# The rotary split of head group 0 in the four softmax buffers, and half of the second gated unit ahead of the first attention

## The chip, the cores and the metric

The kernel runs on one core of one Trainium2 chip, as one program. The metric is the device time of a run in microseconds (us); of several runs the median counts. Lower is better.

## What is computed

The reference is a two-layer backbone over 1024 latent tokens and 256 context tokens, 1024 channels wide. Layer 0 mixes with mLSTM heads and Fourier groups, layer 1 with differential attention and a convolution module; behind each mixer stands a squared-ReLU feed-forward part. The change lies in layer 1's mixer:

```python
q, k, v, glu = jnp.split(h @ w_in, [D_C, 2 * D_C, 3 * D_C], axis=-1)
ql = apply_rope(ql, cos, sin); kl = apply_rope(kl, cos, sin)
s = jnp.einsum('bqhmd,bkhmd->bhmqk', q, k) * (DIFF_DH ** -0.5)      # m = 0, 1: two maps per head
a = softmax(s)[:, :, 0] - lam * softmax(s)[:, :, 1]
o = jnp.einsum('bhqk,bkhd->bqhd', a, v)                             # then an RMS norm per head
a, gte = jnp.split(glu, 2, axis=-1)
z = depthwise_conv(a * jax.nn.sigmoid(gte), w_dw)                   # 31 taps; then layer norm and silu
```

There are six heads, each with two maps of 64 channels and a value of 128. Queries are the 1024 latent tokens, keys and values those and the 256 context tokens.

## The kernel before, in words

**Numbers.** Float32 products are made from pairs: an operand is split into a high part `hi` (rounded to the float32r type) and a low part `lo = x - hi`, and one product is three matmuls (hi by hi, hi by lo, lo by hi: L129, L130, L131). A product over 1024 channels is 8 x 3 = 24 matmuls into one accumulator bank `acc`, of which there are three. Activations are kept as pairs for three token blocks (512, 512 and 256 tokens). Weights come in by SP's queue (`st`, three buffers, L97), ScalarE makes `wah` (L110) and VectorE `wal` (L111).

**Heads in groups.** The six heads are done in three groups of two. For a group, `rope_proj` (its lines are L1016 and on) makes K and then Q. For each token block it makes two products, one for each half of the rotation pairs (A and B). For the latent blocks VectorE then does six operations on the two banks: L1035 (A times cosine), L1036 (B times sine), L1037 (their difference: half 0 is ready), L1038 (A times sine: bank A is read for the last time), L1039 (B times cosine: bank B is free) and L1041 (their sum: half 1 is ready). The tables of cosine (`rc`) and sine (`rs`) have one buffer each, and are loaded anew for each block (L1033, L1034).

**The split.** `to_stack` splits a finished half: ScalarE writes `hi` (L1011), VectorE `lo` (L1012), and SP stores each to a scratch tensor in DRAM, `kd` or `qd` (L1014). The tag `rh` has two buffers for all of this, one pair. A store of a block of 512 tokens is 256 KB, with a destination of 4 x 32 x 512.

**Attention.** `attention` loads K (L1072, 640 KB a map, three buffers) and Q (L1077) back from the scratch. For each block of 128 queries it makes S for both maps (L1086: two matmuls for each of three stretches of keys), the maxima (L1088, L1091), the exponentials into the buffers `p0` and `p1` (L1094; two of each, 1280 columns), the weighted difference (L1101), ten transposes (L1107), the product with the values (L1112), a norm, and a store (L1125).

**The convolution module.** `glu(m)` loads two weight tiles and makes the gated unit of 128 channels: for each of the two latent blocks a product for the gate, a tanh (L969), a product for the value, and their product into `u` (L971). `conv` is one VectorE operation and 30 more over 1024 columns (L976, L978).

**What sets the order.** The kernel is written once, in order; a scheduler then deals the instructions to the engines' queues by a model of their times, so later matmuls stand between those of a stage that waits. Each engine works through its queue in order, and SP's queue, which issues all of these DMAs, stops at a DMA whose data are not there. The written order here is: values of group 0, `glu(0)`, K and Q of group 0, `conv(0)`, attention of group 0, `glu(1)`, K and Q of group 1, values of group 1, `conv(1)`, attention of group 1, and so on.

Of the kernel before, what the change touches and what calls it, by code (L numbers as in the profile page):

```python
# [10 lines left out]
F32R = mybir.dt.float32r  # L11
# [6 lines left out]
P = 128  # L18
# [3 lines left out]
NTOK = T_LAT + T_CTX  # L22
# [20 lines left out]
def body(tc, A, out):  # L43
    with ExitStack() as es:
        trunk(tc, es, A, out)
# [6 lines left out]
def trunk(tc, es, A, out):  # L52
# [12 lines left out]
    def f(ap):  # L65
        return ap.bitcast(F32)
# [13 lines left out]
    def acc(w=512):  # L80
        t = psa.tile([P, 512], F32, tag="acc", name="acc")
        return t[:, :w]
# [31 lines left out]
    def wload(src, shape, pl=None, tag="wa", bufs=3):  # L114
        return wsplit(wstage(src, shape), shape, pl, tag, bufs)
# [20 lines left out]
    def proj(ps, w, h, order=range(KT)):  # L136

        for n, k in enumerate(order):
            mm3(ps, (w[0][:, k, :], w[1][:, k, :]), h[k], n == 0, n == KT - 1)
# [200 lines left out]
    with ExitStack() as em, eg:  # L340
# [57 lines left out]
        for src, dst in ((LI, RI), (LF, RF)):  # L398
            for c0 in range(0, NCH, 4):
                n = min(4, NCH - c0)  # L400
# [428 lines left out]
    with ExitStack() as ef:  # L829
# [30 lines left out]
        for fo in range(5):  # L860
            w = ws[fo] if fo < 2 else wload(A["w_out0"][fo], (KT, P))
            for tb in (0, 1, 2):
                o, n = TBS[tb]
# [65 lines left out]
    pc = er.enter_context(tc.tile_pool(name="proj1", bufs=1, side="right", reuse_waits="tile"))  # L929
# [23 lines left out]
    def hk(tb):  # L953
        return [h1[k, tb] for k in range(KT)]
# [3 lines left out]
    def glu(m):  # L958
        wg = wload(A["w_glu"][2 + m], (KT, P))
        wa = wload(A["w_glu"][m], (KT, P))  # L960
        u = pc.tile([P, T_LAT + 30], F32, tag="uz", bufs=3, name="uz")
        nc.any.memset(u[:, 0:15], 0.0)
        nc.any.memset(u[:, T_LAT + 15:], 0.0)
        for tb in (0, 1):
            o = TBS[tb][0]
            pg_, pa_ = acc(), acc()
            proj(pg_, wg, hk(tb))
            t = pc.tile([P, 512], F32, tag="rt", bufs=3, name="rt")
            act.activation(t, pg_, AF.Tanh, scale=0.5)  # L969
            proj(pa_, wa, hk(tb))  # L970
            dve.scalar_tensor_tensor(u[:, 15 + o:15 + o + 512], t, 1.0, pa_, ADD, MUL)  # L971
        return u

    def conv(m, u):
        zm = pc.tile([P, T_LAT + 30], F32, tag="uz", bufs=3, name="uz")[:, 0:T_LAT]
        dve.tensor_scalar(zm, u[:, 0:T_LAT], dwh[:, m:m + 1], None, MUL)  # L976
        for j in range(1, 31):
            dve.scalar_tensor_tensor(zm, u[:, j:j + T_LAT], dwh[:, 2 * j + m:2 * j + m + 1], zm, MUL, ADD)  # L978
        z.append(zm)
# [26 lines left out]
        yield  # L1006

    def to_stack(dst, g, half, t, o, n, sc):
        hi = pc.tile([P, 512], F32R, tag="rh", bufs=2, name="rh")[:, :n]
        lo = pc.tile([P, 512], F32R, tag="rh", bufs=2, name="rh")[:, :n]  # L1010
        act.activation(hi, t, AF.Copy, scale=sc)  # L1011
        dve.scalar_tensor_tensor(lo, t, sc, f(hi), MUL, SUB)  # L1012
        for kind, s in ((0, hi), (1, lo)):
            sp.dma_start(f(dst[g, :, kind, half, :, o:o + n]), f(s))  # L1014

    def rope_proj(g, q):  # L1016
        w = [wload(A["w_qk1"][q, g, half], (KT, P)) for half in range(2)]
        dst, sc = (kd, 1.0) if q else (qd, 0.125)
        for tb in ((0, 1, 2) if q else (0, 1)):
            o, n = TBS[tb]  # L1020
            pA, pB = acc(n), acc(n)
            proj(pA, w[0], hk(tb))
            proj(pB, w[1], hk(tb))
            t = [pc.tile([P, 512], F32, tag="rt", bufs=3, name="rt")[:, :n] for _ in range(3 if tb < 2 else 2)]
            if tb == 2:
                act.copy(t[0], pA)
                act.copy(t[1], pB)
                to_stack(dst, g, 0, t[0], o, n, sc)
                to_stack(dst, g, 1, t[1], o, n, sc)
                yield  # L1030
                continue
            c_, s_ = (pc.tile([P, 512], F32, tag=x, bufs=1, name=x) for x in ("rc", "rs"))
            sp.dma_start(c_, A["rope"][0, :, o:o + n])  # L1033
            sp.dma_start(s_, A["rope"][1, :, o:o + n])  # L1034
            dve.tensor_mul(t[0], pA, c_)  # L1035
            dve.tensor_mul(t[1], pB, s_)  # L1036
            dve.tensor_sub(t[2], t[0], t[1])  # L1037
            dve.tensor_mul(t[0], pA, s_)  # L1038
            dve.tensor_mul(t[1], pB, c_)  # L1039
            to_stack(dst, g, 0, t[2], o, n, sc)  # L1040
            dve.tensor_add(t[0], t[0], t[1])  # L1041
            to_stack(dst, g, 1, t[0], o, n, sc)
            yield

    def v_proj(g):
        wv = [wload(A["w_v1"][g][:, a:a + 4, :], (4, 256)) for a in (0, 4)]
        v = {}
        for c in (0, 1, 2, 3, 8, 9, 4, 5, 6, 7):
            tb, off = tok(c)
            ps = acc(256)  # L1050
            for kk in range(KT):
                w = wv[kk // 4]
                mm3(ps, tuple(t[:, off:off + P] for t in h1[kk, tb]),
                    (w[0][:, kk % 4, :], w[1][:, kk % 4, :]), kk == 0, kk == KT - 1)
            vt = pv.tile([P, 256], F32, tag="v", bufs=13, name="v")
            act.copy(vt, ps)
            v[c] = vt
        return v
# [69 lines left out]
    pt = e1.enter_context(tc.tile_pool(name="att", bufs=1, reuse_waits="tile"))  # L1128
    def qk_proj1(g):
        for q in (1, 0):  # L1130
            for _ in rope_proj(g, q):
                pass

    v = v_proj(0)
    u = [glu(0)]
    qk_proj1(0)
    conv(0, u[0])
    for _ in attention(0, v, False):
        pass
    u.append(glu(1))  # L1140
    qk_proj1(1)
    v = v_proj(1)
    conv(1, u[1])
    for _ in attention(1, v, False):
        pass
    parts = {"K": rope_proj(2, 1), "Q": rope_proj(2, 0), "0": layernorm_silu(0), "1": layernorm_silu(1)}
# [338 lines left out]
    for j in range(3, 15):  # L1485
        u = up_unit(j)
        u.run(*WORDER)
        u.store()
    u = up_unit(15, False, LORDER)
# [39 lines left out]
    for seg in segs:  # L1529
        tb, a, n = seg  # L1530
# [87 lines left out]
```

## Time and profile before

| | us |
|---|---|
| median of 3 runs | 3104.14 |
| lowest and highest | 3098.87, 3105.69 |
| the profiled execution's own time | 3095.96 |
| its span, from the first to the last instruction | 3094.2 |

The profile is of one execution; times in it are us from the span's start. TensorE is PE, its weight loads PEld, VectorE DVE, ScalarE ACT, GpSimd POOL, and SP issues the DMAs. A row of a timeline has start, duration, engine, line, operation, and in brackets the idle time before it with what ended it; matmuls overlap, so their pace is read from their starts. DMA share is the mean busy share of the core's 16 DMA engines.

### The profile page before, as it was taken

How to read it: one execution, taken by the hardware profiler on the slowest of the kernel's cores; microseconds unless marked ns; L12 is line 12 of the kernel's file. 1: busy time of each engine (PE TensorE's matmuls, PEld its weight loads, DVE VectorE, ACT ScalarE, POOL GpSimd, SP SyncE). 2: the span in 40 equal slices, each digit the busy share in tenths (PEclk: the TensorE clock that was granted, in tenths of full speed). 3: DMA queues.
4: the chain of work that ended last, by engine and by line, in shares of the span. 5: the costliest groups of instructions: out<-in, count | busy, mean ns of one | idle time of the engine just before them, and what ended most of it. 6: DMA issues, size and time to landing. Idle time of an engine off the chain costs nothing.

```text
span 3094.2 us, 44658 instructions
## 1 busy us (share of the span) xinstructions
PE 2933.4 (95%) x16386; PEld 2461.5 (80%) x16386; DVE 1959.3 (63%) x3885; ACT 1205.1 (39%) x2660; POOL 306.0 (10%) x483
## 2 busy tenths in 40 slices
PE   6899999999999999999999799999999799989998
PEld 5787878788888888888888677877877578867787
DVE  6859696646456544544446788567567776657666
ACT  3335354433321222222233145566666454433332
POOL 0002011001122222222100000000000000000000
PEclk9999999999999999999999899999999899999999
DMA  6143334551244444444321333232613386697751
GB/s 214 45 155 108 111 115 136 175 180 55 96 150 158 157 151 141 170 157 164 129 83 63 112 108 109 80 89 82 197 60 109 110 275 233 231 306 236 240 178 65
DMA packets 303803, 443.52 MB, mean 143 GB/s; under 512 B 25712, under 2 KB 174816, under 8 KB 303584
## 3 DMA queue, kind: packets, MB, share of 16 engines
q1 hardware_dynamic: 300992, 436.74, 43.4%
q10 hardware_dynamic: 2592, 3.93, 0.4%
q8 instruction: 129, 2.11, 0.3%
q14 instruction: 90, 0.74, 0.1%
HBM read 330.08 MB, written 110.49 MB: 142 GB/s over the span
## 4 chain that ended last, share of the span: by engine, by line
PE 73%; DVE 11%; DMA 9%; POOL 2%; ACT 2%; issue 2%; SPq 1%; POOLq 0%; DVEq 0%; ACTq 0%
PE acc L131 11%; PE acc L129 11%; PE acc L130 11%; PE acc L1314 8%; PE bd L1314 6%; PE ff L129 4%; PE ff L130 4%; PE ff L131 4%; PE po L1112 3%; PE S L1086 3%; DMA st<-in_ff_dram 2%; DMA kd<-rh 2%; PE pT L1107 2%; DMA qd<-rh 1%; DMA t<-sw 1%
## 5 line engine op out<-in xcount | busy, mean ns | idle before, releaser
L129 PE MATMUL acc<-a,wah 128*128 128x512 f32 (+1 forms) x1752 | 650.1, 371 | 22.4 <-DVE rt L1038 14.1
L130 PE MATMUL acc<-a,wah 128*128 128x512 f32 (+1 forms) x1752 | 644.6, 368 | 0.0
L131 PE MATMUL acc<-a,wal 128*128 128x512 f32 (+1 forms) x1752 | 643.4, 368 | 0.0
L129 PEld LDWEIGHTS acc<-a,wah 128*128 128x128 f32 x1752 | 336.0, 192 | 72.2 <-DVE rt L1038 14.7
L131 PEld LDWEIGHTS acc<-a,wal 128*128 128x128 f32 x1752 | 336.0, 192 | 47.5 <-DVE wal L111 0.6
L130 PEld LDWEIGHTS acc<-a,wah 128*128 128x128 f32 x1752 | 336.2, 192 | 45.6 <-issue 0.5
L110 ACT CAST wah<-st 128x1024 fp32r<-128x1024 f32 (+4 forms) x129 | 120.4, 935 | 483.2 <-DMA st<-in_ff_dram 375.1
L129 PE MATMUL ff<-s,wbh 128*128 128x512 f32 (+1 forms) x768 | 274.3, 359 | 0.2 <-DVE x L710 0.2
L130 PE MATMUL ff<-s,wbh 128*128 128x512 f32 (+1 forms) x768 | 272.4, 355 | 0.0
L131 PE MATMUL ff<-s,wbl 128*128 128x512 f32 (+1 forms) x768 | 271.6, 354 | 0.0
L111 DVE TENSOR_TENSOR wal<-st,wah 128x1024 fp32r<-128x1024 f32 (+4 forms) x129 | 139.3, 1083 | 202.9 <-ACT wah L110 202.6
L710 DVE SCALAR_TENSOR_TENSOR x<-ff,mod,x 128x512 f32<-128x512 f32 (+1 forms) x264 | 171.0, 658 | 96.1 <-PE ff L131 94.8
L1088 DVE TENSOR_REDUCE mx<-S 128x1 f32<-128x512 f32 (+1 forms) x288 | 165.6, 594 | 68.8 <-PE S L1086 67.3
L1094 ACT ACTIVATE p<-S,nm 128x512 f32<-128x512 f32 (+1 forms) x288 | 176.0, 620 | 45.7 <-DVE nm L1091 45.4
L1086 PE MATMUL S<-K,Q 128*128 128x512 f32 (+1 forms) x576 | 164.6, 386 | 15.7 <-ACT p L1094 7.1
L753 DVE TENSOR_TENSOR s<-s,s 128x512 fp32r<-128x512 f32 (+1 forms) x96 | 64.7, 680 | 167.9 <-ACT s L752 167.8
L1314 PE MATMUL bd<-a,wbh 128*128 128x512 f32 x480 | 153.9, 401 | 15.6 <-ACT wbh L1265 8.5
L129 PE MATMUL acc<-wah,a 128*128 128x256 f32 (+1 forms) x560 | 161.8, 290 | 6.5 <-ACT a L271 4.1
L129 PEld LDWEIGHTS ff<-s,wbh 128*128 128x128 f32 x768 | 144.8, 189 | 24.5 <-DVE x L710 1.0
L130 PEld LDWEIGHTS ff<-s,wbh 128*128 128x128 f32 x768 | 145.2, 189 | 20.7 <-DVE s L753 0.6
L131 PEld LDWEIGHTS ff<-s,wbl 128*128 128x128 f32 x768 | 144.9, 189 | 20.8
L131 PE MATMUL acc<-wah,a 128*128 128x256 f32 (+1 forms) x560 | 159.6, 290 | 0.3 <-DVE a L272 0.2
(391 smaller groups left out, 5913.1 us busy)
## 6 DMA issues: line engine op xcount, KB each, us to landing
st<-in_ff_dram SPq DMA_DIRECT2D x168, 256.0 KB
st<-in_ff_dram SPq DMA_DIRECT2D x68, 512.0 KB
st<-in_w_mod_dram SPq DMA_DIRECT2D x48, 512.0 KB
a<-sw SPq DMA_DIRECT2D x84, 256.0 KB
stm<-in_w_mod_dram SPq DMA_DIRECT2D x128, 128.0 KB
su<-st SPq DMA_DIRECT2D x32, 512.0 KB
bc<-rb SPq DMA_DIRECT2D x30, 512.0 KB
sv<-st SPq DMA_DIRECT2D x28, 512.0 KB
```

What stands on the lines that cost most here:

```text
L110: act.copy(hi, v)
L111: dve.tensor_sub(lo, v, f(hi))
L129: pe.matmul(ps, lh, rh, start=first, stop=False)
L130: pe.matmul(ps, lh, rl, start=False, stop=False)
L131: pe.matmul(ps, ll, rh, start=False, stop=last)
L710: dve.scalar_tensor_tensor(xt, ps, mod[:, self.l, ch, fo, s:s + 1], xt, MUL, ADD)
L753: dve.tensor_sub(lo, r, f(hi))
L1086: pe.matmul(s_, Q[m][:, kind, qb * P:(qb + 1) * P], K[hh, m][:, a:a + n], start=(kind == 0), stop=(kind == 1))
L1088: dve.tensor_reduce(mx[:, i:i + 1], s_, AX, MAX)
L1094: act.activation(e[:, a:a + n], S[i], AF.Exp, bias=nm, accum_out=Z[:, m, i:i + 1])
L1112: pe.matmul(po[:, 0:P], aT[:, (c - c0) * P:(c - c0 + 1) * P], v[c][:, hh * P:(hh + 1) * P], start=(c == 0), stop=(c == NCH - 1))
L1314: pe.matmul(ps, l_, r_, start=bool(first) and j == 0 and i == 0, stop=j == n - 1 and i == 2, skip_group_check=True)
```

## The change

`to_stack` takes its pair, for group 0 only, from the attention's buffers `p0` (half 0) and `p1` (half 1): a buffer of 1280 columns holds `hi` in its first n columns and `lo` from column 512 on. So group 0 has four pairs, two for each half, instead of one. Groups 1 and 2 keep `rh`. And `glu` hands out its tile after each token block, so that the main order can run it in two parts: the first block of `glu(1)` is now written ahead of the attention of group 0, the second behind it.

```diff
-        return u
+            yield u
...
     def to_stack(dst, g, half, t, o, n, sc):
-        hi = pc.tile([P, 512], F32R, tag="rh", bufs=2, name="rh")[:, :n]
-        lo = pc.tile([P, 512], F32R, tag="rh", bufs=2, name="rh")[:, :n]
+        if g == 0:
+            hl = pt.tile([P, NTOK], F32R, tag=f"p{half}", bufs=2, name="rp")
+            hi, lo = hl[:, :n], hl[:, 512:512 + n]
+        else:
+            hi, lo = (pc.tile([P, 512], F32R, tag="rh", bufs=2, name="rh")[:, :n] for _ in range(2))
         act.activation(hi, t, AF.Copy, scale=sc)
         dve.scalar_tensor_tensor(lo, t, sc, f(hi), MUL, SUB)
...
     v = v_proj(0)
-    u = [glu(0)]
+    *_, u0 = glu(0)
     qk_proj1(0)
-    conv(0, u[0])
+    conv(0, u0)
+    g1 = glu(1)
+    next(g1)
     for _ in attention(0, v, False):
         pass
-    u.append(glu(1))
+    u1 = next(g1)
     qk_proj1(1)
     v = v_proj(1)
-    conv(1, u[1])
+    conv(1, u1)
```

In the changed file the lines of `to_stack`, `rope_proj` and `attention` have numbers higher by 3: L1038 becomes L1041, L1014 becomes L1017.

TensorE's order around the first S of group 0. The names `a_154..` are activations of token block 0, `a_158..` of block 1; the rows here are of the half unit's products. Two places of the difference:

```order
 L129 MATMUL acc<-a_15496,wah 128x512
 L130 MATMUL acc<-a_15497,wah 128x512
-L1086 MATMUL S<-K,Q 128x512 x2
-L1086 MATMUL S<-K,Q 128x256
 L131 MATMUL acc<-a_15496,wal 128x512
 L129 MATMUL acc<-a_15447,wah 128x512
...
 L131 MATMUL acc<-a_15496,wal 128x512
+L1089 MATMUL S<-K,Q 128x512 x4
+L1089 MATMUL S<-K,Q 128x256 x2
 L129 MATMUL acc<-a_15823,wah 128x512
 L130 MATMUL acc<-a_15824,wah 128x512
```

The first S matmuls stood inside the half unit, three of them one matmul before the end of its first product and three in the middle of its second (34 of its 48 matmuls are ahead of those); now both products are done before the first S.

SP's order from K's last stores to the loads of Q, before:

```order
L1014 DMA kd<-rh 4x32x256 x4
L1072 DMA K<-kd 128x1280 x2
L1014 DMA qd<-rh 4x32x512 x2
L1033 DMA rc<-in_rope_dram 128x512
L1034 DMA rs<-in_rope_dram 128x512
L1014 DMA qd<-rh 4x32x512
L1072 DMA K<-kd 128x1280
L1014 DMA qd<-rh 4x32x512
L1077 DMA Q<-qd 64x512 x3
```

and now:

```order
L1017 DMA kd<-rp 4x32x256 x4
L97 DMA st<-in_w_qk_dram 128x1024 x2
L1075 DMA K<-kd 128x1280 x3
L1017 DMA qd<-rp 4x32x512
L1037 DMA rs<-in_rope_dram 128x512
L1036 DMA rc<-in_rope_dram 128x512
L1017 DMA qd<-rp 4x32x512 x3
L1080 DMA Q<-qd 64x512 x6
```

The third K load has moved up to the first two, ahead of the first store of Q and of the tables for Q's second block; two weight loads stand ahead of them all.

VectorE's order for K's token block 1, now:

```order
L1015 SCALAR_TENSOR_TENSOR rp<-rt,rp 128x512
L1038 TENSOR_TENSOR rt<-acc,rc 128x512
L978 SCALAR_TENSOR_TENSOR uz<-uz,dwh 128x1024 x2
L1039 TENSOR_TENSOR rt<-acc,rs 128x512
L978 SCALAR_TENSOR_TENSOR uz<-uz,dwh 128x1024
L1040 TENSOR_TENSOR rt<-rt 128x512
L978 SCALAR_TENSOR_TENSOR uz<-uz,dwh 128x1024
L1041 TENSOR_TENSOR rt<-acc,rs 128x512
```

Before, one convolution step (L978) stood between the first two of these rotary operations, and two ahead of the split in the first row; now it is two and one.

## Rows read from the trace of the kernel before

**Rows 1.** The page's first section: busy us, share of the span and instructions of each engine.

```profile
PE 2933.4 (95%) x16386; PEld 2461.5 (80%) x16386; DVE 1959.3 (63%) x3885; ACT 1205.1 (39%) x2660; POOL 306.0 (10%) x483
```

**Rows 2.** Busy time by stretch: from:to, us, busy us of each engine (instructions), granted TensorE clock as a share of full speed, DMA share, GB/s.

```profile
1700.00:1800.00 100.00, 78.23 (x335) 64.55 (x334) 67.03 (x77) 14.48 (x26) 0.00 (x0) 0.88 0.38 121
...
1800.00:2390.00 590.00, 559.60 (x3419) 468.30 (x3418) 421.45 (x895) 365.18 (x1030) 40.13 (x51) 0.99 0.33 102
```

**Rows 3.** TensorE's timeline from the end of K's last product to the first attention block; the bracket holds the idle time before a row and what ended it.

```profile
1726.81 0.28 PE L130 MATMUL acc<-a,wah 128*128 128x256 f32 x1
1726.93 0.28 PE L131 MATMUL acc<-a,wal 128*128 128x256 f32 x1
1734.63 0.58 PE L129 MATMUL acc<-a,wah 128*128 128x256 f32 x1 [7.42 <-DVE rt L1038]
...
1735.23 0.41 PE L131 MATMUL acc<-a,wal 128*128 128x256 f32 x1
1735.44 0.41 PE L129 MATMUL acc<-a,wah 128*128 128x256 f32 x1
...
1763.38 0.80 PE L129 MATMUL acc<-a,wah 128*128 128x512 f32 x1 [6.67 <-DVE rt L1038]
...
1764.40 0.63 PE L131 MATMUL acc<-a,wal 128*128 128x512 f32 x1
1764.83 0.63 PE L129 MATMUL acc<-a,wah 128*128 128x512 f32 x1
...
1782.83 1.41 PE L1086 MATMUL S<-K,Q 128*128 128x512 f32 x3 [6.49 <-DMA Q<-qd]
...
1788.73 0.75 PE L1086 MATMUL S<-K,Q 128*128 128x512 f32 x3
1789.31 0.39 PE L131 MATMUL acc<-a,wal 128*128 128x512 f32 x1
1789.54 0.40 PE L129 MATMUL acc<-a,wah 128*128 128x512 f32 x1
...
1798.61 0.73 PE L1086 MATMUL S<-K,Q 128*128 128x512 f32 x2 [1.18 <-ACT p L1094]
```

**Rows 4.** Who waited for whom in 1716 to 1800, TensorE and then VectorE: us in total, times, longest.

```profile
PE acc L129 <- DVE rt L1038: 14.1, 2, 7.4
...
DVE rh L1012 <- DMA qd<-rh: 12.9, 3, 5.6
DVE rh L1012 <- DMA kd<-rh: 11.8, 4, 5.8
```

**Rows 5.** The chain of waits that ended last, in order of time: start, us, what.

```profile
1719.12 8.68 DMA kd<-rh
...
1764.55 8.10 DMA qd<-rh
```

**Rows 6.** Busy time by short stretch, columns as in rows 2; the last two are DMA share and GB/s.

```profile
1721.00:1722.00 1.00, 1.00 (x6) 0.84 (x5) 1.00 (x1) 0.00 (x0) 0.00 (x0) 1.00 0.43 154
1722.00:1723.00 1.00, 1.00 (x6) 0.84 (x5) 0.10 (x1) 0.00 (x0) 0.00 (x0) 1.00 0.26 88
1723.00:1724.00 1.00, 1.00 (x6) 0.81 (x6) 0.00 (x0) 0.00 (x0) 0.00 (x0) 1.00 0.35 121
1724.00:1725.00 1.00, 1.00 (x9) 0.96 (x8) 0.00 (x0) 0.63 (x1) 0.00 (x0) 1.00 0.25 98
...
1750.00:1752.00 2.00, 2.00 (x10) 1.66 (x9) 0.00 (x0) 0.00 (x0) 0.00 (x0) 1.00 0.26 101
...
1764.00:1766.00 2.00, 2.00 (x6) 1.62 (x5) 2.00 (x3) 0.00 (x0) 0.00 (x0) 0.50 0.99 392
```

**Rows 7.** VectorE's timeline at K's token block 1; a convolution step (L978) and a rotary operation give their pace by the next start.

```profile
1719.50 2.60 DVE L978 SCALAR_TENSOR_TENSOR uz<-uz,dwh 128x1024 f32<-128x1024 f32 x2
1727.90 0.69 DVE L1012 SCALAR_TENSOR_TENSOR rh<-rt,rh 128x512 fp32r<-128x512 f32 x1 [5.81 <-DMA kd<-rh]
1728.51 0.68 DVE L1035 TENSOR_TENSOR rt<-acc,rc 128x512 f32<-128x512 f32 x1
1729.11 1.28 DVE L978 SCALAR_TENSOR_TENSOR uz<-uz,dwh 128x1024 f32<-128x1024 f32 x1
```

**Rows 8.** The timeline of SP's queue, which issues the DMAs: start and us of the issuing (not of the transfer).

```profile
1716.68 0.61 SPq L1014 DMA_DIRECT2D kd<-rh  x1
...
1718.41 0.66 SPq L1033 DMA_DIRECT2D rc<-in_rope_dram  x1
...
1761.27 0.81 SPq L1072 DMA_DIRECT2D K<-kd  x2
...
1777.97 1.80 SPq L1077 DMA_DIRECT2D Q<-qd  x3
```

**Rows 9.** ScalarE's timeline: the split of half 1 of K's token block 0, which waits for the store of half 0.

```profile
1724.05 0.63 ACT L1011 ACTIVATE rh<-rt 128x512 fp32r<-128x512 f32 x1 [7.40 <-DMA kd<-rh]
```

**Rows 10.** Whom TensorE waited for in 1800 to 2390: us in total, times, longest.

```profile
PE po L1121 <- ACT ob L1120: 9.9, 11, 2.2
PE pT L1107 <- DVE p L1101: 6.3, 4, 2.9
PE S L1086 <- ACT p L1094: 5.9, 6, 2.1
...
PE acc L986 <- DVE rt L1038: 0.7, 1, 0.7
```

## The prediction

> **What bounds the kernel now.** The page's first section puts TensorE at 95% of the span [rows 1], so a change can only gain where TensorE stands still or runs at the low clock. The busy table by stretch says where that is near this change: in 1700 to 1800 us TensorE is busy 78.23 of 100 us at a mean granted clock of 0.88; in 1800 to 2390, the rest of the attention part, it is busy 559.60 of 590 at 0.99 [rows 2]. So the stretch is 1700 to 1800: the rotary projections of group 0 and the start of its attention.
>
> TensorE's timeline there shows four stops: 7.42, 6.67, 6.49 and 1.18 us [rows 3]. After each long one the matmuls start at the lower of the two clock levels: 128x256 matmuls then follow each other by 0.21 us instead of 0.12, 128x512 ones by 0.43 instead of 0.23 [rows 3]. The slow stretches hold 24 of the narrow ones after the first stop, some 10 wide ones after the second and 11 wide plus three S products after the third: 2.2 + 2.0 + 2.4 = 6.6 us. Stops and low clock together are 21.8 + 6.6 = 28.4 us.
>
> Who is waited for: twice VectorE's L1038 [rows 3, 4], once the load of Q, once an exponential [rows 3]. VectorE itself sits 24.7 us in L1012 (11.8 and 12.9) until a store to kd or qd lands [rows 4]. The chain of waits runs store after store, 8.1 to 8.7 us each from issue to landing [rows 5]: with two "rh" buffers, one hi/lo pair, the next half can't be split before the last pair has landed. L1038 frees an accumulator bank, so TensorE stands still behind that chain.
>
> **What the change does here, step by step.** No matmul, VectorE or ScalarE operation is added or taken away; buffers and order change. I step through the new order with durations from the rows: a rotary operation holds VectorE 0.60 us, a convolution step 1.20 [rows 7], 24 wide matmuls take 24 x 0.227 = 5.4 us, 24 narrow ones 2.9 at full clock.
>
> *K, token block 1 (first stop).* Before, L1035 of block 1 started at 1728.51, right after the split that waited for the store until 1727.90 [rows 7]. Now the split of half 1 has its own pair, and VectorE is free at about 1721. It then waits for something else: the rotary tables have one buffer each, and are reloaded behind the first hi store, the second of them at 1718.41 [rows 8]. When they land no row says. Bounds: 1721 (VectorE free) and 1728.5 (L1035 ran then). Near the lower end would need tables that pass the store; the DMA share says otherwise: it is 0.43 from 1721, then 0.26, 0.35, and from 1724 on 0.25 with 98 GB/s, which is what a store alone shows [rows 6]. So I take 1725. From there to the end of L1041 (today's L1038) it is four rotary operations and four convolution steps, 7.3 us: 1732.4. TensorE, out of work at 1727.2, stands 5.2 us instead of 7.4, with 2.2 us of low clock after.
>
> *Q, token block 0 (second stop).* TensorE now ends K at 1737.5 (24 narrow at 0.21), Q block 0 at 1748.4, the first half of Q block 1 at 1753.8, and then wants the bank that L1041 of Q block 0 frees. VectorE starts that block at 1743.2 (the first product is there at 1742.9) and needs 4 x 0.60 + 6 x 1.20 = 9.6 us: 1752.8. The stop goes, and its 2.0 us of low clock; 1.0 us is to spare.
>
> *Half a gated unit (third stop).* Q block 1 ends at 1759.3, the first product of the half unit at 1764.7. The second wants the bank of L1041 of Q block 1, and that waits for the tables again. On SP they now stand behind three K loads, and these wait for all twelve kd stores. A lone store shows 256 KB at 101 GB/s with a DMA share of 0.26 [rows 6], so 2.6 us each once they stand in a row; on the quarter of the engines that it uses, a table takes 0.65. The first store of K block 1 goes out at about 1731.2, behind L1040 and its copy on ScalarE, and lands 7.4 later, as the very first did (issued at 1716.68, waited for until 1724.05) [rows 8, 9]: 1738.6; two tables, three stores of 256 KB and four of 128 KB behind it are 1.3 + 7.8 + 5.2: 1752.9. Three K loads of 640 KB at 392 GB/s [rows 6] take 5.0, with 1.5 until the engines fill: 1759.5. A qd store and the two tables, 3.9: 1763.4. L1038 to L1041 with three convolution steps and one weight split, 7.1: 1770.5. So TensorE stands 5.9 us, now in the half unit, and loses 2.0 more at the low clock: 1778.0.
>
> *First S.* Behind the tables three qd stores land by 1771.2. Today S starts 4.9 us after the first load of Q was issued (1777.97 and 1782.83) [rows 3, 8]: 1776.1, before 1778.0. No wait, with 1.9 to spare. The six S matmuls end at 1779.2. Today the same work, projections, half a unit and the first S, ends at 1792.3: the last three S matmuls start at 1788.73, thirteen wide ones follow [rows 3]. That is **13.1 us** earlier. The 1.18 us behind it goes too: today the three maxima of S stand between convolution steps on VectorE; now they follow each other.
>
> *The rest of attention.* The order is dealt anew to the end of group 2's attention, with the same work. TensorE's waits there are 30.4 us in 590 [rows 2], the largest for the squares and the copy of the output block (9.9), the weighted difference (6.3) and the exponential (5.9) [rows 10]; for an accumulator it waits 0.7. The half unit taken ahead leaves less cover there, but only 14 of its 48 matmuls stood behind the first S products before: 3.2 us. I put the sum at no change and its bounds at 6 us either way.
>
> **Sum.** 13.1 + 1.2 = 14.3 us. The profiled execution took 3095.96 us (span 3094.2), so it would become 3081.7; it lies 8.2 below the median of the runs, 3104.14. From the median: **3089.8 us**. A measurement here tells about 0.2% (6.2 us) from no change.
>
> **The rivals.**
> *A, the burst of stores buys nothing* (0.16). The stores share their quarter of the engines, so twelve issued early may end no earlier than today, when the K loads went out at 1761.27 [rows 8]. Then the tables land at 1772.5, L1041 at 1779.6, and the third stop becomes 15 us. Stops and clock are 24.4 instead of 15.3, the gain 5: 3099. For it: where only stores run the share is 0.25 or 0.26 [rows 6]. Against: today VectorE waits between them [rows 4].
> *B, the tables come early* (0.07). If stores held nothing up, the first stop would shrink to 1.3 us, VectorE would reach Q block 1 in time, and nearly all of 28.4 us would come back: some 26, 3078. Against it: 8.1 to 8.7 us a store [rows 5] and the quarter share [rows 6]. In the Trainium skill, DMA: Bandwidth & Descriptors, section Anatomy of one DMA, the fit of 2.0 us plus bytes over 436 GB/s (measured on the GpSimd path) would give an estimate of 2.6 us for such a store from issue to landing, and with it this rival's time. The same page of the Trainium skill, section Why a DMA increments its semaphore by 16 and not by 1, has a copy run on as many of the 16 engines as divide the slowest dimension of both sides, four for a destination of 4x32x512; the share of 0.26 agrees, and by that the sum is mine.
> *C, attention waits more* (0.13). The same order that fills the start leaves the blocks behind less covered; if the 30.4 us grow by a quarter, 7.6, the gain is 6.7: 3097. For it: 7,869 rows of TensorE's order differ. Against: only 3.2 us of cover move.
> *D, slower: stores in a row don't overlap* (0.04). SP stops at the K loads until the last kd store lands, and qd stores, tables and loads of Q stand behind. If each 256 KB took the 8.7 us of the chain's rows even in a burst, kd would end at about 1804, the tables would land at 1815 and the half unit end at 1829, 51 us after my 1778: some 37 slower, 3141. It decides from where five such stores' time (three whole, four half) eats 14.3 us: (13.0 + 14.3) / 5 = 5.5 us each. Against it: from 1724 to 1725 a quarter of the engines was still at 98 GB/s when the first store had landed and the next was in flight [rows 6, 9], so the next had not waited for it.
> That the order doesn't do what was meant is excluded by its rows: both products of the half unit stand ahead of the first S.
>
> **How the numbers follow.** My forecast has 0.60, with a range of its own of 3084 to 3096: gains of 8 to 20, from the tables' bounds (2 to 4 us each way), the 1.0 and 1.9 us to spare, and 6 us in attention. For 8 in 10 the range takes in A and C: **3080 to 3101**; beyond it are D, much of B and the ends of the others. Faster by over 0.2%: nearly all of the forecast, B, and parts of A and C, 0.70. Within: the rest of A and C, 0.25. Slower: D and a rough attention, 0.05.
>
> **What would show it.** Right: VectorE no longer waits for kd or qd in the splits; TensorE's second stop is gone, one of about 5 us stays ahead of K's last product and one of 5 to 6 stands inside the half unit, released by L1041; first S near 1778; no store-by-store chain. Wrong: a stop of 10 us or more in the half unit (A), none (B), waits of 36 us or more behind 1800 (C), K loads after 1765 (D).

## The result, and the profile after

The changed kernel takes **3086.1 us** (median of 5 executions, 3081.27 to 3089.09) against 3104.14 (3098.87 to 3105.69): ratio 0.9946, 95% interval 0.9931 to 0.9960, so 16.8 us faster (12 to 21). The forecast was 14.3 us faster, 3089.8. Measured once more, beside the later experiments, it took 3084.15, ratio 0.9948 (0.9933 to 0.9962).

The two profiled executions differ by less, 3095.96 and 3086.10, since the one of before lies 8 us below its own median. They also reach the changed stretch at different times, with the same instructions ahead of it. I therefore count between two points that both have, called marks here. The first mark is the first store to kd (1716.68 before [rows 8], 1720.30 after). The second is the end of SP's issuing of the attention's last output store, ha. That second mark, in SP's timeline of before:

```profile
2381.37 8.18 SPq L1125 DMA_DIRECT2D ha<-oo  x2
```

and of after, with the other issues that count here (start, us of issuing):

```profile
1720.30 0.61 SPq L1017 DMA_DIRECT2D kd<-rp  x1
...
1757.20 1.27 SPq L1075 DMA_DIRECT2D K<-kd  x3
1759.70 0.44 SPq L1036 DMA_DIRECT2D rc<-in_rope_dram  x1
...
2371.05 8.21 SPq L1128 DMA_DIRECT2D ha<-oo  x2
```

From mark to mark it is 672.87 us before and 658.96 after: **13.9 us** of gain, all of it in this part. Behind the second mark 704.7 us are left before and 705.1 after. The busy table from mark to mark, before and then after (start:end, length, busy us and instructions of TensorE, weight load, VectorE, ScalarE, GpSimd, granted clock, DMA share, GB/s):

```profile
1716.68:2389.55 672.87, 620.70 (x3675) 518.66 (x3674) 474.22 (x957) 377.41 (x1052) 40.13 (x51) 0.97 0.34 106
```

```profile
1720.30:2379.26 658.96, 615.21 (x3675) 514.38 (x3674) 474.60 (x957) 379.07 (x1052) 44.90 (x51) 0.98 0.34 108
```

The same 3675 recorded matmuls stand in both. TensorE's idle time falls from 52.2 to 43.75 us, 8.4 less, and the matmuls themselves take 5.5 us less, at a mean granted clock of 0.98 instead of 0.97. Together these are the 13.9.

TensorE's timeline of after in the changed stretch, with all its stops of over 0.5 us and the first S (in brackets: idle time, and what ended it), answers to [rows 3]:

```profile
1736.58 0.58 PE L129 MATMUL acc<-a,wah 128*128 128x256 f32 x1 [5.74 <-DVE rt L1041]
...
1776.82 0.77 PE L129 MATMUL acc<-a,wah 128*128 128x512 f32 x1 [7.31 <-DVE rt L1041]
...
1783.83 1.31 PE L1089 MATMUL S<-K,Q 128*128 128x512 f32 x6
...
1790.23 0.63 PE L1089 MATMUL S<-K,Q 128*128 128x512 f32 x2
```

Four stops of 21.8 us have become two of 13.05. The first S waits for nothing, nor do the next ones up to 1800. Who is waited for in 1716 to 1800, against [rows 4] (us, times, longest):

```profile
PE acc L129 <- DVE rt L1041: 13.1, 2, 7.3
...
DVE rt L1038 <- DMA rc<-in_rope_dram: 12.2, 2, 8.0
```

VectorE's 24.7 us of waiting for stores in the split are gone. In their place it waits for the rotary tables, twice, and its timeline shows that these two waits stand ahead of TensorE's two stops:

```profile
1729.13 0.69 DVE L1038 TENSOR_TENSOR rt<-acc,rc 128x512 f32<-128x512 f32 x1 [4.12 <-DMA rc<-in_rope_dram]
...
1747.79 0.69 DVE L1038 TENSOR_TENSOR rt<-acc,rc 128x512 f32<-128x512 f32 x1
...
1769.46 0.69 DVE L1038 TENSOR_TENSOR rt<-acc,rc 128x512 f32<-128x512 f32 x1 [8.04 <-DMA rc<-in_rope_dram]
```

The rest of the attention, from behind the first S products to the second mark, against the last 590 us of [rows 2]:

```profile
1790.00:2379.00 589.00, 558.30 (x3422) 466.47 (x3420) 421.84 (x894) 366.37 (x1030) 44.90 (x51) 0.99 0.33 103
```

TensorE is idle for 30.7 us there, before for 30.4 in 590.

### The profile page after: what moved, and what is told of

Read it like the earlier page. It is cut to its first block, busy times and chain, and to the rows that moved or that the text cites. A ratio compares the mean times of both kernels' runs of the same rounds, so it can differ in the third digit from the quotient of the medians.

```text
span 3084.4 us, 44653 instructions
## 1 busy us (share of the span) xinstructions
PE 2931.9 (95%) x16386; PEld 2461.1 (80%) x16386; DVE 1957.8 (63%) x3885; ACT 1207.1 (39%) x2660; POOL 310.1 (10%) x483
## 5 line engine op out<-in xcount | busy, mean ns | idle before, releaser
L129 PE MATMUL acc<-a,wah 128*128 128x512 f32 (+1 forms) x1752 | 649.6, 371 | 22.0 <-DVE rt L1041 13.1
L1089 PE MATMUL S<-K,Q 128*128 128x512 f32 (+1 forms) x576 | 161.5, 379 | 11.5 <-ACT p L1097 11.5
L130 PE MATMUL acc<-wal,a 128*128 128x256 f32 (+1 forms) x560 | 161.8, 290 | 0.0
```

Source lines behind the costliest of these rows:

```text
L129: pe.matmul(ps, lh, rh, start=first, stop=False)
L130: pe.matmul(ps, lh, rl, start=False, stop=False)
L1089: pe.matmul(s_, Q[m][:, kind, qb * P:(qb + 1) * P], K[hh, m][:, a:a + n], start=(kind == 0), stop=(kind == 1))
```

## The experiments

Gain below is one less the ratio, times the median of before in the same batch (3104.14 for the change; 3101.61 for e1, e2, e3 and e5; 3100.84 for r, e4, e6 and e7; 3101.11 for e8 to e11). "Mark to mark" and the idle time of TensorE in it come from each run's one profiled execution. They tell where time went; for how much, the medians count: the changed kernel's two traces agree to 0.2 us, but e2's is 3.8 us longer than that of before, though its median is 1.9 us lower. In the runs with four-part stores in the later groups, 10 or 13 matmuls more than the 3675 lie between the marks, since the second mark falls later in TensorE's order there (in e8 and e9 that is 2 to 3 us of TensorE's work).

| run | median us | ratio (95%) | gain us | mark to mark | TensorE idle |
|---|---|---|---|---|---|
| before | 3104.14 | | | 672.9 | 52.2 |
| the change | 3086.10 | 0.9946 (0.9931 to 0.9960) | 16.8 | 659.0 | 43.8 |
| r_after_again | 3084.15 | 0.9948 (0.9933 to 0.9962) | 16.1 | 658.8 | 43.8 |
| e1_buffers | 3093.87 | 0.9974 (0.9963 to 0.9984) | 8.1 | 669.6 | 49.9 |
| e2_half | 3099.46 | 0.9994 (0.9986 to 1.0003) | 1.9 | 676.7 | 53.1 |
| e3_tables | 3080.13 | 0.9929 (0.9916 to 0.9942) | 22.0 | 657.5 | 41.1 |
| e5_before_spread | 3087.79 | 0.9951 (0.9939 to 0.9964) | 15.2 | 657.1 | 39.7 |
| e4_after_spread | 3082.65 | 0.9941 (0.9926 to 0.9956) | 18.3 | 655.9 | 36.7 |
| e7_after_spread_first | 3090.83 | 0.9968 (0.9957 to 0.9980) | 9.9 | 665.4 | 44.6 |
| e6_tables_spread | 3080.39 | 0.9934 (0.9919 to 0.9949) | 20.5 | 655.6 | 36.8 |
| e8_after_spread_later | 3069.59 | 0.9895 (0.9882 to 0.9909) | 32.6 | 647.0 | 29.4 |
| e9_tables_spread_later | 3067.03 | 0.9888 (0.9875 to 0.9902) | 34.7 | 641.5 | 25.8 |
| e10_before_spread_first | 3087.48 | 0.9951 (0.9937 to 0.9964) | 15.2 | 658.4 | 46.8 |
| e11_before_spread_later | 3091.04 | 0.9967 (0.9955 to 0.9980) | 10.2 | 662.9 | 42.0 |

My theory was that one store of a hi or lo half holds the only buffer pair, that the splits therefore run store after store, and that with more buffers the tables behind the stores hold next. The main rival was that it is the work order (half a unit ahead) that gains, or that the stores hold nothing.

**e1_buffers**: the four softmax buffers, the second gated unit whole behind the first attention.

```diff
-    g1 = glu(1)
-    next(g1)
     for _ in attention(0, v, False):
         pass
-    u1 = next(g1)
+    *_, u1 = glu(1)
```

> Only the four softmax buffers for group 0's split; the gated unit stays behind the attention. Theory (the store-by-store chain was the cost, the tables and the wait for Q are what is left): the stops of VectorE for kd and qd go, TensorE keeps a stop of 5 to 6 us before K's last product, loses the second one, and waits some 8 us for the first S, at about the time at which the changed kernel stands inside the half unit; so 11 to 16 us faster than before, at most 3 us less than the whole change. Rival (the half unit ahead is what pays): within 5 us of before.

**e2_half**: only the half unit ahead; every split keeps the one rh pair.

```diff
-        if g == 0:
-            hl = pt.tile([P, NTOK], F32R, tag=f"p{half}", bufs=2, name="rp")
-            hi, lo = hl[:, :n], hl[:, 512:512 + n]
-        else:
-            hi, lo = (pc.tile([P, 512], F32R, tag="rh", bufs=2, name="rh")[:, :n] for _ in range(2))
+        hi, lo = (pc.tile([P, 512], F32R, tag="rh", bufs=2, name="rh")[:, :n] for _ in range(2))
```

> Only the first half of the second gated unit ahead of the first attention; the split keeps one pair of buffers for all groups. Theory: the two stops behind the accumulator banks stay (7.4 and 6.7 us), of the 6.5 us at the first S some 4 go since the half unit's second product fills them, so 3 to 6 us faster than before. Rival (the half unit is what pays): 12 us or more faster.

Both fell short of what was expected, 8.1 and 1.9 us (the interval of e2 takes in no change at all), and their sum is under the whole's 16 to 17. The timeline of e1 says why:

```profile
1732.13 0.58 PE L129 MATMUL acc<-a,wah 128*128 128x256 f32 x1 [5.76 <-DVE rt L1041]
1773.32 1.40 PE L1089 MATMUL S<-K,Q 128*128 128x512 f32 x3 [11.52 <-DMA Q<-qd]
```

The stop of 5.76 us at K is that of the whole change, and the second stop is gone as there. But without the half unit TensorE arrives early at the first S, and waits 11.5 us there for Q. In e2 the chain of stores stays, and its stops with it:

```profile
1737.46 0.58 PE L129 MATMUL acc<-a,wah 128*128 128x256 f32 x1 [7.45 <-DVE rt L1037]
1766.28 0.79 PE L129 MATMUL acc<-a,wah 128*128 128x512 f32 x1 [7.27 <-DVE rt L1037]
1783.44 0.77 PE L129 MATMUL acc<-a,wah 128*128 128x512 f32 x1 [4.48 <-DVE rt L1037]
```

The wait of 6.49 us for Q [rows 3] is gone, but a stop of 4.48 us behind the splits stands in the half unit instead. So the halves of the change need each other: the buffers make TensorE early, and only the half unit has work for the time until Q is there.

**e3_tables**: the whole change, and the tables of token block 1 of group 0 in the attention's `aT` buffers, so that their loads need not wait for those of block 0 to be used up.

```diff
+            if g == 0 and tb == 1:
+                c_, s_ = (pt.tile([P, 512], F32, tag="aT", bufs=3, name=x) for x in ("rc", "rs"))
+            else:
                 c_, s_ = (pc.tile([P, 512], F32, tag=x, bufs=1, name=x) for x in ("rc", "rs"))
```

> The whole change, and for group 0 the rotary tables of token block 1 lie in the attention's aT buffers, so that a table needn't wait for the one before it. Theory (the tables, queued behind stores and K loads, hold what stops are left): both stops at the banks go (5.7 and 7.3 us with some 4 us of low clock in the changed kernel); a stop at the first S comes in their place, 4 to 7 us, since Q still waits for K's stores; 8 to 12 us faster than the changed kernel, 24 to 30 faster than before. Rival (the stores' own pace sets the end of the stage, whatever the tables do): within 4 us of the changed kernel.

The tables did hold both stops: one shrinks to 1.53 us, the other is gone. But only 5 to 6 us of the expected 8 to 12 came out, because the next wait was already standing behind. Its timeline, at the first S:

```profile
1773.78 0.77 PE L1092 MATMUL S<-K,Q 128*128 128x512 f32 x1 [6.95 <-DMA Q<-qd]
...
1776.54 2.07 PE L1092 MATMUL S<-K,Q 128*128 128x512 f32 x5 [1.99 <-DMA Q<-qd]
```

The 13.05 us of stops have become 10.5, most of them for Q. The size stays uncertain: the intervals of the two ratios overlap, and the trace of e3 is only 1.5 us shorter from mark to mark.

**e5_before_spread**: the kernel before, with each store to kd and qd issued as four of 32 partitions (the destination is 4x32x512).

```diff
-            sp.dma_start(f(dst[g, :, kind, half, :, o:o + n]), f(s))
+            for j in range(4):
+                sp.dma_start(f(dst[g, j, kind, half, :, o:o + n]), f(s[32 * j:32 * j + 32]))
```

> The kernel before, with each 256 KB store to kd or qd issued as four of 64 KB (32 partitions each), in all groups. Theory (a store with a destination of 4 x 32 x 512 runs on a quarter of the engines, and its time is what the one pair of buffers waits for): the DMA share rises over 0.5 while stores run, a link of the chain falls from 8.1-8.7 us to 4-6, VectorE's waits for kd and qd from 24.7 us to under 12, and the kernel is 8 to 16 us faster than before. Rival (a store's time is latency, not the quarter of the engines): links of 8 us stay, SP's issuing is added, same or slower.

As expected: 15.2 us, without any of the change, and kd and qd are gone from the list of what VectorE waits for in the stage. Its first stop is longer than before, 10.46 us, its second is gone, and the third is 6.36. Whether the 15.2 us come from the place where the change works, the other runs had to tell.

**r_after_again**, the changed kernel beside the next three:

> The changed kernel once more, on the chip of the three runs below, so that they are read against it. 3081 to 3091 us, ratio to the kernel before 0.993 to 0.997; TensorE stops of 5 to 6 and 7 to 8 us on the rotary sine product, none for Q at the first S, and 30 to 31 us of TensorE idle in the attention.

As expected, with stops of 5.67 and 7.42 us and no wait for Q at the first S.

**e4_after_spread** (the edit of e5 on the changed kernel) and **e7_after_spread_first** (the same for `g == 0` alone):

> The changed kernel with every store to the rotary stacks issued as four of 32 partitions. In the kernel before this was worth 15 us; what it adds to the change tells how far both take away the same thing. Theory 1 (the chain of stores was the cost that both remove, tables and Q are then held by the stores still on their way): the four-part stores leave sooner, the tables' stops of 5.7 and 7.3 us lose 2 to 4 us each: 4 to 8 us below the changed kernel. Rival 2 (SP's issue takes the place: in the kernel before with four-part stores 16 of them took 10.40 us of SP's time, and the tables behind them made a stop of 10.46 us): the first stop grows to about 10, the second goes to 6: 0 to 4 us above the changed kernel, unless rival 3 holds as well. Rival 3 (part of the 15 us came in the attention, whose TensorE idle time was 22.9 us against 30.2 before): a further 7 us below, whatever the stage does.

> The changed kernel with the four-part stores in the first head group alone; those of the two later groups are whole again. The stage as in the run with all stores split, within 1 us. Rival 3 (the splits of the later groups relieve the attention or what follows it): 5 to 9 us above that run. Theory 1 and rival 2: the same time as that run within 3 us, since all they speak of lies in the first group.

Theory 1 is wrong here; rivals 2 and 3 both hold, rival 2 with 6.2 us where it put 0 to 4. In the first group alone the four-part stores cost the changed kernel 6.2 us by the gains of the table, and those of the later groups give 8.4 back. From mark to mark e7 has 6.4 us more than the change, of which only 0.9 is idle time; the rest is matmul time at a lower mean clock (TensorE busy 620.7 instead of 615.2, granted 0.97 instead of 0.98). In the timeline of e7 the first stop has nearly doubled, and the second has shrunk from 7.31:

```profile
1739.15 0.58 PE L129 MATMUL acc<-a,wah 128*128 128x256 f32 x1 [10.46 <-DVE rt L1045]
1765.66 0.80 PE L129 MATMUL acc<-a,wah 128*128 128x512 f32 x1 [4.82 <-DVE rt L1045]
```

SP's timeline names the cause of the longer stop: sixteen issues stand ahead of the tables. The cosine table went out 1.7 us behind the first store in the changed kernel, and goes out 8.9 us behind it here. That this stop also makes the whole of the 6 us is not shown: part of the low clock comes far behind it, in the attention (granted 0.93 in 1850 to 1920, in the changed kernel 1.00).

```profile
1718.15 8.89 SPq L1019 DMA_DIRECT2D kd<-rp  x16
1727.09 0.42 SPq L1040 DMA_DIRECT2D rc<-in_rope_dram  x1
```

**e6_tables_spread**: e3 and the four-part stores in all groups.

> The changed kernel with the tables of token block 1 in the attention's aT buffers and the four-part stores together. With the tables alone Q at the first S was waited for 8.9 us and the time was 3080 us. Theory 1: Q's stores leave sooner and the wait falls to 2 to 5 us: 3073 to 3077. Rival 2 (SP's issue of four times as many stores comes ahead of the K and Q loads): the wait stays at 8 to 12 us: 3079 to 3084. Rival 3 takes 7 us from either.

3080.4, no better than e3 alone: rival 2's time, without the 7 us of rival 3. The wait for Q is gone, as theory 1 has it, but a stop of 9.8 us on the rotary sine product is there again. With the first group's stores whole (e9, below) the same kernel is 14 us faster.

**e8_after_spread_later** and **e9_tables_spread_later**: the changed kernel, and e3, with `if g > 0:` ahead of the four-part stores.

> The changed kernel with the four-part stores in the two later head groups only, which still go through the pair of rh buffers. Theory (the four-part stores in the first group cost the changed kernel 6 to 7 us through SP's issue, and in the later groups gain about 8 by ending the chain of stores that lies in the first attention): 6 to 10 us below the changed kernel, 3074 to 3078, with TensorE busy over 97 us of 1800 to 1900 (91.8 in the changed kernel) and the stops before S as in the changed kernel. Rival (what the later groups gained depends on the first attention's start, which the four-part stores of the first group shift): 0 to 4 us below.

> As the run before, and with the tables of token block 1 in the attention's aT buffers. If the parts add up (tables 4 to 5 us, later four-part stores 8): 3070 to 3074. Rival (the Q wait of 8.9 us at the first S, or the attention that starts sooner, takes one back): 3076 to 3080.

Both did better than any theory said: 32.6 and 34.7 us, twice the change's gain. The stage up to S is that of the changed kernel (5.71 and 7.48 us of stops in e8). The gain lies where the rotary splits of the later groups run between the blocks of the attention, still through the rh pair. Who waited in 1800 to 1950 of the changed kernel:

```profile
ACT rh L1014 <- DMA kd<-rh: 8.4, 4, 2.8
...
PE po L1124 <- ACT ob L1123: 6.1, 9, 3.0
PE S L1089 <- ACT p L1097: 4.8, 3, 1.7
DVE rh L1015 <- DMA qd<-rh: 3.5, 1, 3.5
DVE rh L1015 <- DMA kd<-rh: 3.0, 1, 3.0
ACT rh L1014 <- DMA qd<-rh: 2.8, 1, 2.8
```

ScalarE and VectorE stand 17.7 us for those stores, with the exponentials and copies of the attention queued behind them, and TensorE behind these. In e8 no such wait is left; busy time of the same stretch, the changed kernel and then e8:

```profile
1800.00:1950.00 150.00, 136.70 (x824) 113.50 (x822) 126.58 (x239) 86.35 (x247) 14.20 (x12) 0.99 0.35 104
```

```profile
1800.00:1950.00 150.00, 147.84 (x927) 125.14 (x927) 133.73 (x255) 94.29 (x274) 13.85 (x13) 1.00 0.35 100
```

TensorE works 11.1 us more of 150. It doesn't end there: the changed kernel's splits through rh run on to 2160, and ScalarE and VectorE stand 30.1 us for stores of them in all (18.4 for kd, 11.7 for qd), in e8 not at all. In 1950 to 2250 TensorE works another 9.1 us more in e8 (294.1 instead of 285.0 of 300). The same chain of stores that the change takes out of the first group was alive in the later ones. Parts don't add up strictly: the tables are worth 5.9 us on the changed kernel and 2.1 on e8, though the intervals overlap in both pairs. By their medians e9 is the fastest version here.

**e10_before_spread_first** and **e11_before_spread_later**: the kernel before, with the four-part stores for `g == 0` and for `g > 0` alone.

> The kernel before with the four-part stores in the first head group alone. Of the 15 us that they gained in all groups, theory: 6 to 9 us lie in the first group (the chain of stores goes, SP's issue comes in its place), so 3092 to 3096. Rival (all of the gain lies in the later groups): 3099 to 3104, though the chain of stores is gone from the trace.

> The kernel before with the four-part stores in the two later groups alone. Theory: the other 6 to 9 us, so 3092 to 3096, with the stage up to the first S as before. Rival: all 15, 3085 to 3088.

15.2 and 10.2 us, where 6 to 9 were expected of each, and 15.2 of both together: either one takes most of what there is. e11 leaves the first group as it was, stops of 7.41, 7.80 and 6.13 us, and still gains. e10 comes to the change's own time by another way (stops of 10.46 and 6.48 us, none between them), and with the change added to it (e7) gains nothing more, rather 5 us less. So the chain of stores in the first group is what the change removes; where four-part stores have already ended the chain, its buffers and its order bought nothing here. What keeps e5 from the sum of e10 and e11 I have not found. In the traces the gains in idle time nearly add up, 5.4 and 10.2 us against 12.5; those in the matmuls' own time don't, 9.1 and -0.1 against 3.3. No run shows why.

## Why the prediction was right, point by point

Times are from the first store, forecast and then measured.

- *What bounds the kernel.* Right: 12.0 of the 13.9 us came in the stage and right behind it.
- *K, token block 1.* The chain goes, and the tables hold: the stop was put at 5.2 us, it is 5.74. TensorE goes on at 15.7, measured 16.3. The table was in use at 8.8 where I chose 8.3.
- *Q, token block 0.* The stop is gone, as worked out.
- *Half a gated unit.* The stop stands where it was put, behind the tables behind the K loads: 5.9 us forecast, 7.31 measured. The K loads go out at 36.9 (36.2), so a run of stores does drain at the quarter-share pace, as the row of after below shows. The mis-sized term is the next one: from the K loads to L1038 I put 10.5 us, it takes 12.3. TensorE goes on at 56.5 instead of 53.8.

```profile
1743.00:1750.00 7.00, 7.00 (x32) 5.78 (x31) 6.13 (x7) 0.63 (x2) 0.00 (x0) 1.00 0.26 102
```

- *First S.* Without a wait, at 63.5 instead of 61.3. The same work as in the forecast's comparison (projections, half a unit, six S products) ends 10.8 us earlier than before, not 13.1. The 1.18 us behind it did go.
- *The rest of attention.* Idle time 30.4 before, 30.7 after: no change, as put. (By the trace 13 of the half unit's matmuls stood behind the first S products before, not 14, which shifts nothing here.) But 1.9 us came from there all the same (13.9 less 10.8 and 1.2): two spells of the lower clock that before has, in 1850 to 1900 and in 1950 to 2000, are not there after. A later one is longer instead (granted 0.93 in 2100 to 2150, before 0.97), so that in sum one spell is saved. The prediction had no term for this. Before, and then after:

```profile
1850.00:1900.00 50.00, 45.58 (x271) 38.00 (x270) 40.98 (x77) 27.57 (x81) 3.33 (x4) 0.97 0.41 122
...
1950.00:2000.00 50.00, 45.46 (x326) 41.43 (x327) 26.50 (x61) 28.70 (x88) 2.70 (x5) 0.97 0.24 76
```

```profile
1850.00:1900.00 50.00, 44.96 (x281) 37.97 (x280) 42.54 (x80) 28.54 (x82) 4.56 (x4) 1.00 0.40 122
...
1950.00:2000.00 50.00, 48.28 (x351) 43.75 (x350) 21.96 (x49) 26.04 (x76) 3.41 (x4) 1.00 0.23 74
```

- *The sum.* 14.3 forecast, 13.9 in the traces: 2.3 us too much in the stage, 1.9 too little behind it. That the sum is closer than its terms are is luck. The medians' 16.8 has an interval of 12 to 21 that holds both; what lies between it and the traces' 13.9 no run shows.
- *The rivals.* A wanted a stop of 10 us or more in the half unit, B none there; it is 7.31. C wanted waits of 36 us or more; they are 30.7. D wanted the K loads later than 48.3 us behind the first store; they go out at 36.9.

What the prediction did not see is the rest of the same mechanism: it took the 30 us of waits in the attention as given, while some 14 of them hang on the rh pair of the later head groups (idle time from mark to mark 43.8 us in the changed kernel, 29.4 in e8).

## What to carry to other kernels

Look for who waits for a store, not only for a load: a buffer pair that is freed by a store ties its splits to the store's landing, and the engines that do the splits pass the wait on to everything queued behind them. When such a chain is broken, list what stands behind it (here tables, then Q) and have independent work ready for the time that is won; half of the change alone gave half or less. And follow a mechanism through every place where the code repeats: the chain left in the later groups was worth as much as the one removed.

## What the runs showed of the hardware

A whole store of 4x32x512 runs alone at a DMA share of 0.26 and 101 GB/s [rows 6]. As four of 32 partitions the same bytes show about twice the share and 105 to 137 GB/s; busy time of e10 while SP issues twelve of them in a row:

```profile
1719.00:1721.00 2.00, 2.00 (x10) 1.67 (x9) 2.00 (x5) 0.00 (x0) 0.00 (x0) 1.00 0.45 105
1721.00:1723.00 2.00, 2.00 (x10) 1.67 (x9) 1.97 (x4) 0.63 (x1) 0.00 (x0) 1.00 0.48 117
1723.00:1725.00 2.00, 2.00 (x10) 1.65 (x10) 1.96 (x2) 0.00 (x0) 0.00 (x0) 1.00 0.57 137
```

SP's issues of the first four, ahead of which the engines were idle (DMA share 0.00 in 1717.0 to 1718.7), and of the last four of the twelve:

```profile
1718.73 1.74 SPq L1016 DMA_DIRECT2D kd<-rh  x4
...
1722.86 1.79 SPq L1016 DMA_DIRECT2D kd<-rh  x4
```

An issue takes 0.44 to 0.45 us whether the engines are idle or not, and 256 KB in 1.79 us would be 146 GB/s, not far above the 137 that the last row shows. So the pace of four-part stores in a row is close to that at which SP issues them. (The 10.40 us that SP's row gives for all sixteen, quoted in an expectation above, hold a pause of 2.8 us in which SP waits for VectorE's last split.) What the four-part stores win is how soon one of them has landed: ScalarE's second split waits for the very first store, and goes on 3.2 us after that was issued (1718.73), where in the kernel before it was 7.4 [rows 8, 9]. In e10:

```profile
1721.96 0.63 ACT L1011 ACTIVATE rh<-rt 128x512 fp32r<-128x512 f32 x1 [3.26 <-DMA kd<-rh]
```

A lone split in the attention gains by that, a burst ahead of waiting loads doesn't: on the changed kernel the same edit gave 16 us in the later groups (e8) and cost 6 in the first (e7).

The Trainium skill, DMA: Bandwidth & Descriptors, section Why a DMA increments its semaphore by 16 and not by 1, would have a copy with 32 as the slowest dimension of both sides on all 16 engines, instead of four; the share of 0.45 to 0.57, against 0.26, agrees in that it is more than four of sixteen engines could show. That SP's pace keeps it from rising further is likely, but no run here issues such stores faster.
